# A 64-byte load on each DMA engine in front of the first tile's load of a gradient kernel

## Chip, cores, metric

One core of one Trainium2 chip. The metric is the device time of one execution in microseconds (us), median of several runs; lower is better. The profile's span is about 2 us shorter than that time and is used for everything inside the kernel.

## The reference

```python
def setup_inputs():
    return {"x": np.random.randn(8192, 8192).astype(np.float32)}

def reference(x):
    return np.gradient(x, axis=1)
```

Each output element is half the difference of its right and left neighbour in the row; the two end columns are plain differences. 268 MB are read and 268 MB written.

## The kernel before

The rows are cut into 32 tiles of 128 partitions x 2 rows (64 KiB per partition, 8 MiB in all), which pass through three slots. A slot starts with 64 spare elements, so that the result can be written 64 elements in front of the data it is made from.

```python
    R = 2; NB = 3; SH = 64; W = R * m; nsets = n // (P * R)          # 32 tiles
    slots = [pool.tile([P, SH + W], f32, ...) for k in range(NB)]
    ends = pool.tile([P, nsets, R, 2], f32, name="ends", tag="ends")

    def load(i):
        b = slots[i % NB]
        ins = nc.sync.dma_start(out=b[:, SH : SH + W], in_=x_sets[i])
        loads.append(chain(i, ins, *([stores[i - NB]] if i >= NB else [])))

    with tc.manual_schedule():
        for i in range(NB):
            load(i)                                   # loads 0, 1, 2
        for i in range(nsets):
            # GpSimd: the two end differences of each row into `ends`; waits for load i
            # VectorE: one custom instruction, half the neighbour difference, in place
            # VectorE or GpSimd: the ends into the result
            last = i == nsets - 1
            nr = 1 if last else R                     # the last tile goes in two halves
            for r in range(0, R, nr):
                ...
                ins = nc.sync.dma_start(out=out_sets[i, ...], in_=b[...])
                stores[i] = chain(i, ins, placed)
            if i % NB == NB - 1:                      # after every third tile
                for k in range(i + 1, min(i + 1 + NB, nsets)):
                    load(k)                           # each waits for the store of its slot
```

`chain` draws the dependences by hand.

Of the kernel before, what the change touches and what calls it, by code (L numbers as in the profile page):

```python
# [1 line left out]

# [4 lines left out]


@with_exitstack
def kernel(  # L10
    ctx: ExitStack,
    tc: tile.TileContext,
    x: bass.AP,
    out: bass.AP,
):










    nc = tc.nc
    P = nc.NUM_PARTITIONS
    n, m = x.shape
    R = 2
    NB = 3  # L30
    SH = 64
    W = R * m
    nsets = n // (P * R)
    f32 = x.dtype

    x_sets = x.rearrange("(s p t) m -> s p (t m)", p=P, t=R)
    out_sets = out.rearrange("(s p t) m -> s p (t m)", p=P, t=R)

    pool = ctx.enter_context(tc.tile_pool(name="pool", bufs=1))
    slots = [pool.tile([P, SH + W], f32, name=f"slot{k}", tag=f"slot{k}") for k in range(NB)]  # L40
    ends = pool.tile([P, nsets, R, 2], f32, name="ends", tag="ends")
    loads, stores = [], [None] * nsets
    in_front = {}

    def chain(i, ins, *needed):



        group, engine = f"slot{i % NB}", ins.ins.engine
        keep = [o.ins for o in needed]  # L50
        if in_front.get(engine, (None,))[0] == group:
            keep.append(in_front[engine][1])
        tc.declare_no_dep(ins.ins, group=group, keep=keep, reason="implied by the needed step")
        tc.add_to_no_dep_group(group, ins.ins)
        in_front[engine] = group, ins.ins
        return ins
# [4 lines that stand above are left out]
        loads.append(chain(i, ins, *([stores[i - NB]] if i >= NB else [])))  # L61

    with tc.manual_schedule():
        for i in range(NB):
            load(i)
        for i in range(nsets):
            b = slots[i % NB]
            xin = b[:, SH : SH + W].rearrange("p (t m) -> p t m", m=m)

            ins = nc.gpsimd.tensor_sub(  # L70
                out=ends[:, i, :, :],
                in0=xin[:, :, 1 : m : m - 2],
                in1=xin[:, :, 0 : m - 1 : m - 2],
            )
            at = [chain(i, ins, loads[i])]
            last = i == nsets - 1
            nr = 1 if last else R
            for r in range(0, R, nr):
                c0, c1 = r * m + 1, (r + nr) * m - 1

                ins = nc.vector._custom_dve(  # L81
                    dve_ops.TENSOR_TENSOR_REDUCE_SUB_MAX,
                    out=b[:, c0:c1],
                    in0=b[:, SH + c0 + 1 : SH + c1 + 1],
                    in1=b[:, SH + c0 - 1 : SH + c1 - 1],
                    s0=0.0,
                    s1=0.5,
                )
                halved = chain(i, ins, *at)
                res = b[:, r * m : (r + nr) * m].rearrange("p (t m) -> p t m", m=m)  # L90
                placer = nc.gpsimd if i % 5 in (1, 3) and not last else nc.vector
                ins = placer.tensor_copy(out=res[:, :, 0 : m : m - 1], in_=ends[:, i, r : r + nr, :])  # L92
                placed = chain(i, ins, halved)
                ins = nc.sync.dma_start(
                    out=out_sets[i, :, r * m : (r + nr) * m], in_=b[:, r * m : (r + nr) * m]
                )
                stores[i] = chain(i, ins, placed)
                at = [halved]
            if i % NB == NB - 1:
                for k in range(i + 1, min(i + 1 + NB, nsets)):  # L100
                    load(k)


# [1 line left out]
_INS = ['x']  # L105
_OUTS = [((8192, 8192), 'float32')]


# [23 lines left out]
```

## Time and profile before

| what | value | from |
|---|---|---|
| time | 1248.15 us median of 3 (1247.39 to 1248.5) | runs |
| span of the profiled run | 1245.0 us | page |
| VectorE busy | 45% | page |
| the DMA queue's packets | 99.8% of 16 engines' span | page |
| a 65,536-byte packet | 2.418 us, 512 per engine | packet records |
| first packets of load 0 | 3.10 us on the mean | packet records |

The kernel is one stream of packets on 16 engines. A packet is what one DMA engine moves in one go, in a load of a tile the 64 KiB of one partition. A 4-byte semaphore packet behind the last of them on each engine reports the end, and a transfer has *landed* when all 16 have done so. SPq is the queue of SyncE that issues transfers.

A line of stretches of time reads: start and end, length, VectorE busy (x instructions), GpSimd busy (x instructions), granted TensorE clock, DMA share, GB/s. A packet is counted with its whole length in the stretch in which it *starts*, so the DMA share can exceed 1, and the share times the length is how long the packets that start there last, per engine. The records do not name the engine of a packet; where the text tells engines apart, it goes by the order of the starts. The lines themselves stand in the prediction.

### The profile page before, as it was taken

The numbers are of one execution on the slowest core, as the hardware profiler recorded it, in microseconds if no ns is written. First come the engines' busy times: TensorE is split into PE (matmuls) and PEld (weight loads), VectorE is DVE, ScalarE is ACT, GpSimd is POOL, SyncE is SP. The second block draws the span as 40 slices with busy tenths as digits, with TensorE's granted clock in tenths as the row PEclk, the third lists the DMA queues.
The fourth block names the chain that finished last, engine by engine and source line by source line (L and its number), as shares of the span: only waits on it lengthen the run. The fifth ranks groups of instructions, "written<-read, shape, count | busy, mean of one in ns | idle before, by whom it ended". The sixth has DMA issues, their size and how long they took to land.

```text
span 1245.0 us, 241 instructions
## 1 busy us (share of the span) xinstructions
DVE 554.8 (45%) x54; POOL 8.8 (1%) x48
## 2 busy tenths in 40 slices
DVE  2850483079009603850582079009603840591083
POOL 0000000000000000000000000000000000000000
DMA  9999999999999999999999999999999999999999
GB/s 404 438 436 419 425 438 438 438 438 438 434 427 421 436 438 438 436 438 432 432 419 438 436 438 432 436 434 432 423 436 436 436 438 436 430 427 430 436 411 404
DMA packets 9361, 536.88 MB, mean 431 GB/s; under 512 B 1040, under 2 KB 1040, under 8 KB 1040
## 3 DMA queue, kind: packets, MB, share of 16 engines
q1 hardware_dynamic: 9360, 536.88, 99.8%
q14 instruction: 1, 0.01, 0.0%
HBM read 268.44 MB, written 268.44 MB: 431 GB/s over the span
## 4 chain that ended last, share of the span: by engine, by line
another core or an unknown queue 74%; DVE 18%; DMA 3%; issue 2%; POOL 1%; SPq 0%; POOLq 0%
DVE slot L81 18%; DMA slot<-in_x_dram 3%; POOL ends L70 0%; POOL slot L92 0%; SPq L60 0%; DVE slot L92 0%; POOLq L127 0%
## 5 line engine op out<-in xcount | busy, mean ns | idle before, releaser
L81 DVE CUSTOM_DVE_ANT_0 slot<-slot 128x16382 f32<-128x16382 f32 (+1 forms) x33 | 551.3, 16706 | 667.9 <-POOL ends L70 667.9
L70 POOL TENSOR_TENSOR ends<-slot 128x4 f32<-128x4 f32 x32 | 6.3, 198 | 988.8 <-DMA slot<-in_x_dram 988.8
L92 DVE COPY slot<-ends 128x4 f32<-128x4 f32 (+1 forms) x21 | 3.6, 172 | 0.7
L92 POOL COPY slot<-ends 128x4 f32<-128x4 f32 x12 | 2.3, 190 | 207.9 <-DVE slot L81 207.9
L116 POOL MEMSET const-bfloat16-1.0<- 128x1 bf16 x1 | 0.1, 102 | 0.0
L116 POOL MEMSET const-uint8-127<- 128x1 uint8 x1 | 0.1, 102 | 0.0
L116 POOL MEMSET const-float32-0.0<- 128x1 f32 x1 | 0.1, 99 | 0.2 <-issue 0.2
L116 POOL MEMSET const-float32-1.0<- 128x1 f32 x1 | 0.1, 99 | 0.0
## 6 DMA issues: line engine op xcount, KB each, us to landing
out_dram<-slot SPq DMA_DIRECT2D x2, 4096.0 KB, 20.2
slot<-in_x_dram SPq DMA_DIRECT2D x32, 58.0
out_dram<-slot SPq DMA_DIRECT2D x31, 40.3
```

The lines of the kernel that those rows point to most:

```text
L70: ins = nc.gpsimd.tensor_sub(out=ends[:, i, :, :], in0=xin[:, :, 1 : m : m - 2], in1=xin[:, :, 0 : m - 1 : m - 2],)
L81: ins = nc.vector._custom_dve(dve_ops.TENSOR_TENSOR_REDUCE_SUB_MAX, out=b[:, c0:c1], in0=b[:, SH + c0 + 1 : SH + c1 + 1], in1=b[:, SH + c0 ...
L92: ins = placer.tensor_copy(out=res[:, :, 0 : m : m - 1], in_=ends[:, i, r : r + nr, :])
L116: nc = _bacc.Bacc("TRN2", target_bir_lowering=False, num_devices=1)
```

## The change

The intent is to let a tiny transfer pay whatever the first transfer on each engine costs, so that the first big load starts at full speed. 16 rows of 64 bytes, one row for each engine; nobody reads them.

```diff
     ends = pool.tile([P, nsets, R, 2], f32, name="ends", tag="ends")
+    few = pool.tile([16, 16], f32, name="few", tag="few")
...
     with tc.manual_schedule():
+
+        nc.sync.dma_start(out=few[:], in_=x[0:16, 0:16])
         for i in range(NB):
             load(i)
```

## The prediction

> **What bounds the kernel now.** I read four views in this order: the page, the waits of the DMA-issuing engine, then stretches of time at the start, at the first store and near the end (with single packets of the trace where a mean was wanted). The page first:
>
> ```profile
> span 1245.0 us, 241 instructions
> ...
> DVE 554.8 (45%) x54; POOL 8.8 (1%) x48
> ...
> q1 hardware_dynamic: 9360, 536.88, 99.8%
> ...
> slot<-in_x_dram SPq DMA_DIRECT2D x32, 58.0
> out_dram<-slot SPq DMA_DIRECT2D x31, 40.3
> ```
>
> VectorE is busy 45% of the span, but one hardware queue holds packets on the 16 DMA engines 99.8% of it. The kernel is a stream of 32 loads and 32 stores (the last store in two halves). A load is 128 rows of 64 KiB, so each engine gets 8 packets of 65,536 bytes; all transfers together make 512 such packets per engine. In the packet records the usual packet takes 2.418 us (the median) and the next starts 2.416 us after it: 512 x 2.416 = 1237 us. Only some 8 us of the 1245 lie outside that, and the change can touch only a part of these.
>
> ```profile
> SPq L94 <- DVE slot L92: 525.7, 21, 55.9
> SPq L60 <- DMA out_dram<-slot: 373.2, 29, 19.2
> ```
>
> SyncE waits for long times, but not with the engines empty: when it waits for a store to free a slot, other transfers are queued (that is why a load takes a median of 58.0 us to land, three times its own 19.3 us). Inside the stream there is thus no idle time that could absorb a shift; a shift at the start goes through to the end. Now the start, in stretches. The last column times the length is the bytes of the packets that *start* in the stretch: 1165 x 0.9 us is 1.05 MB, 16 packets, one per engine.
>
> ```profile
> 0.74 1.33 SPq L60 DMA_DIRECT2D slot<-in_x_dram  x3
> 22.70 0.20 POOL L70 TENSOR_TENSOR ends<-slot 128x4 f32<-128x4 f32 x1 [22.26 <-DMA slot<-in_x_dram]
> ```
>
> ```profile
> 0.00:1.50 1.50, 0.00 (x0) 0.20 (x4) 1.00 0.00 0
> 1.50:2.40 0.90, 0.00 (x0) 0.00 (x0) 1.00 3.44 1165
> 2.40:4.50 2.10, 0.00 (x0) 0.00 (x0) 1.00 0.00 0
> 4.50:5.40 0.90, 0.00 (x0) 0.00 (x0) 1.00 2.69 1165
> 5.40:7.00 1.60, 0.00 (x0) 0.00 (x0) 1.00 0.00 0
> 7.00:7.80 0.80, 0.00 (x0) 0.00 (x0) 1.00 3.02 1311
> ```
>
> Load 0 is issued at 0.74 us; the engines' first packets start between 1.75 and 2.35 us (mean 1.92), the second between 4.62 and 5.37, the third between 7.04 and 7.79. So the first packets took 2.71 to 3.39 us, mean 3.10: **0.68 us more** than 2.42. That is also what the DMA share column shows: 3.44 x 0.9 = 3.10 us per engine against 2.69 x 0.9 = 2.42 for the second. This 0.68 us is the only thing that a load in front can save. (Loads 1 and 2 are issued 0.44 and 0.47 us after the one before.)
>
> A first store has such a cost too, and there the engines were not empty:
>
> ```profile
> 58.10:58.80 0.70, 0.70 (x1) 0.00 (x0) 1.00 4.82 1498
> 58.80:61.40 2.60, 0.69 (x1) 0.19 (x1) 1.00 0.00 0
> 61.40:62.20 0.80, 0.00 (x0) 0.00 (x0) 1.00 3.03 1311
> ```
>
> 4.82 x 0.7 = 3.37 us per engine (with the last load's 4-byte semaphore packets in it), about 0.95 more than 2.42; no later change from loads to stores shows it. A load does not touch this one.
>
> Near the end:
>
> ```profile
> 1186.42 17.23 DVE L81 CUSTOM_DVE_ANT_0 slot<-slot 128x16382 f32<-128x16382 f32 x1 [59.81 <-POOL ends L70]
> 1203.68 0.17 DVE L92 COPY slot<-ends 128x4 f32<-128x4 f32 x1
> 1203.88 19.93 SPq L94 DMA_DIRECT2D out_dram<-slot  x3
> ```
>
> Store 30 can be issued only when load 30 has landed (1186.2) and 17.2 us of VectorE have passed; most engines have then finished load 31 and stand idle, 1.49 us on average, until 1204.7. From there 16 packets per engine (38.7 us) run to 1243.7. This gap is set by when the *slowest* engine lands load 30, and it moves along with the loads, so it does not absorb a shift either.
>
> **What the Trainium skill says.** "DMA: Bandwidth & Descriptors", section "Why a DMA increments its semaphore by 16 and not by 1": the number of engines is the largest number up to 16 that divides the slowest dimension of both sides, so the 16-row load puts one 64-byte row on each of the 16 engines; the 128-row loads of before agree, with 16 first packets. The same page, section "Latency and other measured facts", gives about 600 ns to the first byte and about 800 ns as the least HBM round trip of a tiny transfer; the trace has 1.0 us from the issue to the first packet's start, and the extra 0.68 us of a first packet is of the size of such a trip. Section "Two DMAs through the same engine are not ordered" says that descriptors start in order but are pipelined; the trace agrees in that only the first packet of a long load shows the extra. Section "Where 436 GB/s comes from" puts the ceiling at 435.2 GB/s; 16 x 65,536 bytes per 2.416 us is 434, so the stream has nothing left to gain.
>
> **The change part by part.** It removes nothing. It adds:
> (a) One DMA issue on SyncE in front of load 0. At the measured spacing of first issues, 0.44 us, load 0's issue goes from 0.74 to about 1.18 us. Taking the same 1.0 us and the same spread, its first packets could start at 2.2 to 2.8 us instead of 1.75 to 2.35.
> (b) 16 data packets of 64 bytes and 16 semaphore packets of 4 bytes (9 ns each in the trace). The 64-byte ones start where load 0's first packets start now, 1.75 to 2.35 us. By its size one takes next to nothing; if it has the first packet's extra time, about 0.7 us (an estimate: the 0.68 us above), so they end at 2.45 to 3.05 us.
> (c) 64 bytes of SBUF on 16 partitions, which no instruction reads; no new wait. The DMA semaphores are used in turn, eight of them; every transfer still waits only for the one eight places before it, long done.
>
> If the small packet takes the extra time upon itself, load 0's first packet starts when both its descriptor and the engine are there, 2.45 to 3.05, and lasts 2.42: it ends at 4.87 to 5.47 us. Before, it ended at 4.75 to 5.32 or so. Sum: +0.44 (issue) + 0.26 (the small packet outlasts that by 0.70 - 0.44) - 0.68 (extra saved) = **+0.02 us** by the means, up to +0.14 by the ends of the ranges. So the small load pays the cost a little earlier and the issue slot eats the profit.
>
> **The rivals.**
> 1. *The extra is paid again*: it belongs to starting on an empty pipe, the small packet is gone before load 0's descriptor arrives, and load 0's first packet lasts 3.10 again. Then the whole 0.44 us of the issue is lost: +0.44 us, about 1248.6. For it: 64 bytes are quickly through. Against: the first store shows 0.95 with the pipe full, so the extra looks like a first use rather than an empty pipe.
> 2. *The small load is cheaper than I think*: few descriptors, so it starts at once everywhere, and its 0.68 lies wholly within the 0.44 and the descriptor latency. Then load 0's packets start at 2.2 to 2.8 and last 2.42: 0.44 - 0.68 = -0.24 us, about 1247.9.
> 3. *A small write stalls the engine*, or the semaphore packet behind it holds up the data: some 1 us more, 1249.2. Against: after load 0 the 4-byte packets take 9 ns and load 1 goes on without a gap.
> 4. *The stream falls otherwise into step*: the three runs of before differ by 1.1 us, and the engines' spread is about 2.6 us at load 31's end against 0.6 at the start. That is larger than the effect and can go either way.
>
> **Range and chances.** The cases lie between -0.24 and +1.0 us. I take mine and rival 1 as about equally likely and rival 2 as half as likely: (0.05 x 2 + 0.44 x 2 - 0.24) / 5 = +0.15, so 1248.15 + 0.15 = 1248.3 us. The scatter of the three runs (1247.39 to 1248.5) and of another session is more than this: I add about 1.3 us to each side, 1247.0 to 1249.6. Two per cent are 25 us; nothing in an opening of 5 us can make that. I leave half a per cent on either side.
>
> **What would show it right or wrong.** In the profile after: 32 packets more on the queue (9392); under 512 B 1072; the issue of the first big load about 0.44 us later; the 64-byte packets at about 1.75 to 2.35 us; 16 big packets starting between 2.2 and 3.1 us, and the next 16 at 4.7 to 5.6. If the two are 2.42 us apart, the small load took the extra on itself; if 3.1, rival 1 holds. Load 0's wait should end within 0.5 us of the 22.70 of before, and the first store should keep its 0.95. The prediction is wrong if the time moves by over 1.5 us, or if the shift at load 0 does not appear at the end in runs that are otherwise alike.

## The result

| | before | after |
|---|---|---|
| time, median (4 runs each) | 1248.33 us (1247.39 to 1248.68) | 1248.13 us (1247.87 to 1248.52) |
| span of the profiled run | 1245.0 us | 1246.0 us |

The ratio is 1.0 (95% interval 0.9983 to 1.0017). Ratios here are the mean time of one kernel's fast runs over that of the other's of the same rounds, so not quite the ratio of the medians. The times are the same; what the change did at the start has to be read from the profile. The page after, where it answers to the lines of before:

```profile
span 1246.0 us, 243 instructions
...
q1 hardware_dynamic: 9392, 536.88, 99.7%
...
few<-in_x_dram SPq DMA_DIRECT2D x1, 1.0 KB, 1.5
```

32 packets more, and the small load lands 1.5 us after its issue. The start in order of time, after:

```profile
0.74 0.39 SPq L66 DMA_DIRECT2D few<-in_x_dram  x1
1.18 1.36 SPq L61 DMA_DIRECT2D slot<-in_x_dram  x3
22.95 0.20 POOL L73 TENSOR_TENSOR ends<-slot 128x4 f32<-128x4 f32 x1 [22.51 <-DMA slot<-in_x_dram]
```

The small load takes load 0's place at 0.74 us; load 0 is issued 0.44 us later. The stretches of the start, after:

```profile
1.50:2.10 0.60, 0.00 (x0) 0.00 (x0) 1.00 0.03 2
2.10:3.20 1.10, 0.00 (x0) 0.00 (x0) 1.00 2.71 953
3.20:5.10 1.90, 0.00 (x0) 0.00 (x0) 1.00 0.00 0
5.10:5.70 0.60, 0.00 (x0) 0.00 (x0) 1.00 4.03 1748
```

In the first line are the small packets: 0.03 x 0.60 = 0.02 us per engine for a 64-byte packet and its semaphore packet (8 and 9 ns in the records; the 64-byte ones start at 1.75 to 1.91 us). In the second line are load 0's first packets, one per engine (953 x 1.1 us = 1.05 MB): 2.71 x 1.1 = **2.98 us** each, so still not 2.42. In the last line their successors start, at 5.49 us on the mean of the records against 5.01 before. The small load has saved nothing that can be seen of load 0's slow start, and load 0's data come **0.48 us later**. That is well beyond the scatter: in the seven profiles told of here in which load 0 is issued at 0.74 us, the second packets start at 4.98 to 5.07 us on the mean; in two profiles of the changed kernel at 5.49 and 5.50. The end of the first wait is a poorer measure, as it ends with the slowest engine: 22.95 against 22.70 us here, but 22.61 to 22.94 in those seven profiles.

### The profile page after: what moved, and what is told of

The parts are those of the page before. It is cut to its first block, busy times and chain, and to the rows that moved or that the text cites. A ratio compares the mean times of both kernels' runs of the same rounds, so it can differ in the third digit from the quotient of the medians.

```text
span 1246.0 us, 243 instructions
## 1 busy us (share of the span) xinstructions
DVE 554.8 (45%) x54; POOL 8.9 (1%) x48
## 4 chain that ended last, share of the span: by engine, by line
another core or an unknown queue 74%; DVE 18%; DMA 3%; issue 2%; POOL 1%; SPq 0%; POOLq 0%
DVE slot L84 18%; DMA slot<-in_x_dram 3%; POOL ends L73 0%; POOL slot L95 0%; SPq L61 0%; SPq L66 0%; DVE slot L95 0%; POOLq L130 0%
```

## The experiments

Two quantities are used throughout. The *lead* is the time from load 0's issue until its data flow at full rate: the mean start of the second packets, less one packet's 2.418 us, less the issue. The *rest* is the time from the mean start of the second packets to the end of the last packet of the kernel. In the kernel before the lead is 5.008 - 2.418 - 0.738 = 1.85 us and the rest 1238.7 us; after, 5.489 - 2.418 - 1.181 = 1.89 us and 1239.3 us. (In the seven profiles with load 0 at 0.74 us the lead is 1.83 to 1.91, so 0.04 us means nothing.) My theory after the first profile: the lead is a fixed cost of starting loads on idle engines, the small load only costs its issue slot, and the shift goes through to the end but is smaller than the scatter of the rest. The rivals: a first use that the small load might take on itself if placed or sized otherwise; a slowdown by the following loads' issues; a stream that absorbs the shift.

### Six small loads, and twelve

```diff
-        nc.sync.dma_start(out=few[:], in_=x[0:16, 0:16])
+        for j in range(6):          # or 12
+            nc.sync.dma_start(out=few[:, 16 * j : 16 * j + 16], in_=x[0:16, 16 * j : 16 * j + 16])
```

> Six small loads of 64 bytes per engine in front instead of one. Theory (the issue slot is all that the small load costs, the first packet's extra is not saved, and the shift goes through to the end): load 0 is issued 6 x 0.44 = 2.7 us later than in the kernel before, its landing ends the first wait at about 25.3 us (22.70 before, 22.95 with one), and the time rises by about 2.7 us, to about 1251. Rival (the stream absorbs shifts at the start, as the equal medians could also suggest): the landing moves by 2.7 us but the time by less than 1 us. Rival (small loads warm something up step by step): load 0's first packets last 2.42 us and the time rises by 2.0 us or less.

> Twelve small loads in front. Theory (0.44 to 0.46 us for each, nothing of it absorbed): load 0 is issued 5.4 us later than before, its second packets start at 10.4 to 10.5 us on the mean, and the time rises by 4.9 to 5.9 us. Rival (the stream absorbs part): the time rises by under 4 us. Rival (each small load costs more than its issue slot): over 6.5 us.

In order of time with twelve:

```profile
0.74 5.47 SPq L67 DMA_DIRECT2D few<-in_x_dram  x12
6.25 1.37 SPq L61 DMA_DIRECT2D slot<-in_x_dram  x3
28.29 0.20 POOL L74 TENSOR_TENSOR ends<-slot 128x4 f32<-128x4 f32 x1 [27.84 <-DMA slot<-in_x_dram]
```

| small loads | load 0 issued | second packets, mean | lead | ratio of time (95%) | in us |
|---|---|---|---|---|---|
| none | 0.74 us | 5.01 us | 1.85 us | 1 | 0 |
| 6 | 3.48 | 7.86 | 1.96 | 1.0026 (1.0014 to 1.0039) | +3.2 |
| 12 | 6.25 | 10.59 | 1.92 | 1.0042 (1.0030 to 1.0055) | +5.2 |

("In us" is the ratio less 1, times the median of before.) Twelve small loads shift load 0's data by 5.6 us and the time by 5.2 us; six by 2.9 and 3.2. Each small load costs 0.46 us of issue, and the stream passes the shift to the end. A stream that absorbs the shift is refuted by the six: it asked for under 1 us, and the interval is 1.7 to 4.9 us. With twelve the interval, 3.7 to 6.9 us, holds the shift of 5.6 but just reaches into both rivals (under 4 and over 6.5), so a partial absorption is made unlikely, not excluded; in the profiles the rest is 1238.7 us with none and with twelve. Small loads warm nothing up step by step either: after twelve the lead is still 1.92 us. The second packets were expected at 10.4 to 10.5 us; they came at 10.59, a small miss.

### The small load from another queue

```diff
-        nc.sync.dma_start(out=few[:], in_=x[0:16, 0:16])
+        nc.scalar.dma_start(out=few[:], in_=x[0:16, 0:16])
```

> The same small load issued by ScalarE's queue, so that SyncE's load 0 keeps its place at 0.74 us. Theory (only the issue slot costs): load 0's issue at 0.74 us, first packets of about 3.1 us, landing at 22.7 us as before, time as before within 0.1%. Rival (a first use that the small load takes on itself, eaten up by the issue slot): first packets of about 2.4 to 2.6 us, landing at about 22.0 us, time 0.6 us shorter.

Load 0 is back at 0.74 us, the small load is issued at the same moment by ScalarE, and load 0's second packets start at 4.99 us (5.01 before): lead 1.83 us. The first wait ends at 22.64 us; time 1248.11 us, ratio 0.9999 (0.9986 to 1.0011). Taken off the issue path the small load costs nothing and brings nothing. The records of load 0's first packets last 2.96 us here, a little less than I expected, only because some of them start later; the data do not come earlier. This is why the start of the second packet is the better measure. One thing this run does not test, though the expectation says so, is a first use: in the records the small packets start only at 4.62 to 5.35 us, behind load 0's first packets and not in front of them.

### The small load behind load 0

```diff
+        load(0)
         nc.sync.dma_start(out=few[:], in_=x[0:16, 0:16])
-        for i in range(NB):
+        for i in range(1, NB):
             load(i)
```

> The same small load between load 0 and load 1. Theory (only the issue slot in front of load 0 costs): landing of load 0 at 22.7 us as before, load 1 issued 0.44 us later but hidden behind load 0's 19 us, load 1 landing at 42.0 us as before, time as before within 0.1%. Rival (the extra packets themselves cost engine time): load 1 lands 0.2 us or more later than before.

The second packets start at 5.06 us, the waits for loads 0 and 1 end at 22.68 and 42.02 us (22.70 and 42.04 before); ratio 1.0003 (0.9990 to 1.0015). The 16 small packets pass between the two loads in 11 ns each. So the packets cost nothing; the place in front of load 0 does.

### Load 0 waits for the small load

```diff
-        nc.sync.dma_start(out=few[:], in_=x[0:16, 0:16])
+        small = nc.sync.dma_start(out=few[:], in_=x[0:16, 0:16])
         for i in range(NB):
             load(i)
+            if i == 0:
+                after(loads[0], small)        # load 0 waits until the small load has landed
```

(`after(a, b)` makes `a` wait for the landing of `b`. The later runs use it too.)

> Load 0 waits until the small load has landed (1.5 us from its issue in the profile after), so the engines have done a whole transfer and are idle again when load 0 comes. Theory (the extra belongs to every start of loads on idle engines, not to a first use): the small load's semaphore is full at about 2.25 us, load 0 is issued at about 2.3, its first packets last 3.0 to 3.1 us again, landing at 24.2 to 24.4 us, time about 1.6 us longer. Rival (a first use of engine, ring or memory that needs one finished transfer): first packets of 2.42 us, landing at about 23.6, time about 0.9 us longer.

The stretches of the start:

```profile
1.50:2.10 0.60, 0.00 (x0) 0.00 (x0) 1.00 0.03 2
2.10:3.20 1.10, 0.00 (x0) 0.00 (x0) 1.00 0.00 0
3.20:3.70 0.50, 0.00 (x0) 0.00 (x0) 1.00 6.21 2097
3.70:6.20 2.50, 0.00 (x0) 0.00 (x0) 1.00 0.00 0
6.20:6.80 0.60, 0.00 (x0) 0.00 (x0) 1.00 4.03 1748
```

Here every engine has finished a whole transfer, data and semaphore, before load 0 is issued at 2.24 us. Load 0's first packets last 6.21 x 0.50 = 3.10 us nevertheless, as with no small load at all, and the lead is 1.82 us. The idea of a first use that one finished transfer takes away is refuted. The wait ends at 24.08 us, a little before the 24.2 that I expected at the least, and the time is longer by a ratio of 1.0014 (1.0000 to 1.0028), about 1.7 us.

### A larger load in front

```diff
-    few = pool.tile([16, 16], f32, name="few", tag="few")
+    few = pool.tile([16, 2048], f32, name="few", tag="few")
...
-        nc.sync.dma_start(out=few[:], in_=x[0:16, 0:16])
+        nc.sync.dma_start(out=few[:], in_=x[0:16, 0:2048])
```

> One load in front as in the change, but of 8 KiB on each engine instead of 64 bytes: 0.3 us of transfer at the engines' full rate. Theory (fixed 1.85 us from issue to flow, for the load in front as for load 0): the load in front flows from about 2.6 to 2.9 us, load 0 from about 3.05; the second packets of load 0 start 0.45 to 0.6 us later than before; the 8 KiB packets carry an extra of about 0.7 us themselves (about 1.0 us each) and load 0's first packets carry less of it in their records, but nothing is gained; time as before within 0.1%. Rival (64 bytes are too little to warm an engine, 8 KiB are enough): load 0's second packets start at 5.0 us or sooner.

The 8 KiB packets last 0.32 to 0.59 us, not the 1.0 us that I expected, where full rate would take 0.30; so a small packet's record shows little of the slow start, and mine was the wrong idea of where it would appear. Load 0's second packets start at 5.50 us, as after the change; lead 1.90 us, ratio 1.0002 (0.9988 to 1.0016). More bytes in front do not help either.

### Loads on idle engines in the middle of the program

```diff
                     load(k)
+                    if k == NB:
+                        after(loads[k], stores[NB - 1])     # load 3 also waits for store 2
+                    elif k < 2 * NB:                        # second run only
+                        after(loads[k], loads[k - 1])       # loads 4 and 5 start singly
```

> The kernel before, with load 3 waiting also for store 2, so that loads 3, 4 and 5 are issued one behind the other on engines that have run dry in the middle of the program, 100 us after the first use of everything. Theory A (each start of loads on idle engines costs the extra): load 3's first packets last about 3.0 us, as at the start. Theory B (the extra comes from the next two loads being issued meanwhile): 3.0 us here too, but 2.42 us in the run with single issues. Theory C (something of the first microseconds of the program alone): 2.42 us. Time: engines idle for about 2 us once, plus the extra: 2.0 us longer under C, 2.6 to 2.7 under A and B.

> As the last, and loads 4 and 5 each wait for the landing of the load before, so that three loads start singly on idle engines in the middle. Theory A: the first packets of each last about 3.0 us; time three times 2.7 us, about 8 us longer. Theory B: 2.42 us each, time about 6 us longer. Theory C: 2.42 us each.

The stretches around the three single starts in the second run:

```profile
121.20:122.30 1.10, 0.00 (x0) 0.00 (x0) 1.00 2.83 953
122.30:124.30 2.00, 0.00 (x0) 0.00 (x0) 1.00 0.00 0
124.30:125.00 0.70, 0.00 (x0) 0.00 (x0) 1.00 3.46 1498
143.10:143.70 0.60, 0.60 (x1) 0.00 (x0) 1.00 5.31 1748
143.70:146.10 2.40, 2.40 (x1) 0.00 (x0) 1.00 0.00 0
146.10:147.00 0.90, 0.90 (x1) 0.00 (x0) 1.00 2.69 1165
```

2.83 x 1.10 = 3.11 us and 5.31 x 0.60 = 3.19 us for the first packets of loads 3 and 4, and 3.17 us for those of load 5 (records); the packets after them 2.42 us (2.69 x 0.90). With the three issued together it is 3.10 us. The three leads are 1.85, 1.86 and 1.88 us, the same as at the program's start. So the cost came back at **every** start of loads on idle engines that was tried, also 100 us after the first use of anything, and it does not come from the issues that follow. Theory A holds, B and C fall.

The ratios are 1.0032 (1.0018 to 1.0046) and 1.0071 (1.0057 to 1.0085), about 4.0 and 8.9 us. A said 2.7 and 8; both lie within the intervals (2.2 to 5.7 and 7.1 to 10.6 us), so the times do not show that anything is missing. The traces do have one more difference of about 1 us: the last packets of load 5, just before the stores behind it, last 3.53 and 3.44 us in the two runs, as those of load 2 do in the kernel before (3.37 us), while in the kernel before those of load 5 take 2.42 us and in the other profiles with no such idle start up to 2.78.

### The first loads issued singly

```diff
             load(i)
+            if i > 0:
+                after(loads[i], loads[i - 1])
```

> The kernel before, with load 1 waiting for load 0 and load 2 for load 1 at the start: load 0 is issued alone. Theory A: load 0's first packets last about 3.1 us as before, and those of loads 1 and 2 too; landing of load 0 at 22.7. Theory B: load 0's first packets last 2.42 us, landing at about 22.0. Theory C: load 0's 3.1 us, those of loads 1 and 2 2.42. Time two idle stretches of about 2 us longer, 4 to 5.5 us in all.

Load 0's first packets last 3.07 us though nothing else is issued until 22.68 us, those of loads 1 and 2 3.05 and 3.13; ratio 1.0043 (1.0029 to 1.0057), 5.4 us. Theory A again.

### The changed kernel once more

> The changed kernel itself once more, for a second profile and more times. Theory (a start of loads takes a fixed time of about 1.85 us from the issue until the data flow at full rate, and the small load only moves the issue by 0.44 us): second packets of load 0 start 0.45 to 0.55 us later than in the kernel before, on the mean of the engines; time within 0.1% of before, because the slowest engine's later delays scatter by more than that. Rival (a gain of the change that one profile hid): second packets at 5.01 us or sooner.

No edit. The second packets start at 5.50 us, as in the first profile of the change; lead 1.90 us; ratio 1.0003 (0.9990 to 1.0015), median 1248.46 us. The rest is 1240.7 us here against 1239.3 us in the first profile *of the same kernel*. That is the scatter in which 0.48 us are lost.

### The last tile but one in halves

```diff
-            last = i == nsets - 1
+            last = i >= nsets - 2
```

> The kernel before, with the last tile but one also worked and stored in halves, so that its first half is stored about 8.5 us sooner and the engines need not stand idle at about 1203 us. Theory (the slowest engine sets the end, and that one did not stand idle: it ended load 31 at 1205.05 us, after the others had started store 30 at 1204.73): the idle 1.5 us of the mean disappear, the engines end at different times, and the time falls by less than 0.5 us. Rival (that idle stretch lies on the path): the time falls by 1.5 us.

Near the end of the kernel before:

```profile
1238.00:1239.50 1.50, 0.00 (x0) 0.00 (x0) 1.00 0.81 350
1239.50:1241.00 1.50, 0.00 (x0) 0.00 (x0) 1.00 0.81 350
1241.00:1242.50 1.50, 0.00 (x0) 0.00 (x0) 1.00 1.57 677
1242.50:1244.00 1.50, 0.00 (x0) 0.00 (x0) 1.00 0.06 22
```

and with the halves:

```profile
1238.00:1239.50 1.50, 0.00 (x0) 0.00 (x0) 1.00 1.11 481
1239.50:1241.00 1.50, 0.00 (x0) 0.00 (x0) 1.00 0.61 262
1241.00:1242.50 1.50, 0.00 (x0) 0.00 (x0) 1.00 0.20 87
1242.50:1244.00 1.50, 0.00 (x0) 0.00 (x0) 1.00 0.20 87
1244.00:1245.50 1.50, 0.00 (x0) 0.00 (x0) 1.00 0.05 22
```

Before, 16 packets are in flight until 1243.5 us and all end within 0.2 us. With the halves only eight are in flight at 1241.0 us and four at 1241.5, and the last two packets end at 1245.0 and 1245.4 us. The idle time at 1203 us is gone (1.50 us per engine before, 0.00 here), yet the end is no earlier: the waiting of the other engines for the slowest has moved to the end. The ratio is 1.0001 (0.9987 to 1.0014), that is -1.6 to +1.7 us, which alone would not quite exclude the rival's gain of 1.5 us; what speaks against it is the trace.

No experiment points to a version that beats both kernels.

## Why the prediction was right, point by point

The time, 1248.3 us in a range of 1247.0 to 1249.6, was right: 1248.13 us, and 1248.46 us when measured again. The chance of a change of over 2% was rightly put near nothing. The mechanism that I had put first was not the right one, so that the number came out right is luck as far as that mechanism goes: the range of 2.6 us held my own case (1248.2), rival 1 (1248.6), rival 2 (1247.9) and rival 3 (1249.2) alike, and the time cannot tell them apart.

- **The stream has no idle time to absorb a shift.** Right. With six and twelve small loads the time rose by 3.2 and 5.2 us for shifts of 2.9 and 5.6 us.
- **(a) The issue slot, 0.44 us.** Right: load 0's issue went from 0.738 to 1.181 us.
- **(b) The 64-byte packets.** They start where I put them, from 1.75 us, but do not last 0.7 us: 8 ns. The step of the sum that failed is "- 0.68 (extra saved)". The extra is not a first use that one transfer takes from the next. It came back in full after a landed small load (3.10 us), and in the middle of the program (3.10 to 3.19 us). With nothing saved, and nothing lost to a small packet outlasting the issue, the sum is +0.44 instead of +0.02; measured at load 0: +0.48 and +0.49 us. Two slips in the sums changed little: load 0's first packets ended at 4.62 to 5.37 us before, not "4.75 to 5.32 or so", so the ends of the ranges would have given +0.25 and +0.10 and not "up to +0.14"; and the weighted mean takes 0.05 where the sum gave 0.02, and leaves rival 3 out.
- **Rival 1, "the extra is paid again",** is what happened. I had weighed it equally with my own case, so that the predicted figure, +0.15, lay between.
- **The argument against rival 1** was a misreading. I took the 3.37 us packets at 58.2 us for the first store. They are the 24th of each engine, and three loads make 24 packets of each: 1.92 + 3.10 + 22 x 2.416 = 58.2 us. So they are load 2's *last* packets. And "no later change from loads to stores shows it", from which I took the extra for a first use, is not so. The last packets before later changes are longer too in some places, only less so; at 639 us in the kernel before 1.89 x 1.5 = 2.84 us on the mean:

```profile
639.00:640.50 1.50, 1.50 (x1) 0.00 (x0) 1.00 1.89 699
```

In all thirteen profiles load 2's last packets take 3.33 to 3.80 us on the mean. So the 3.64 us after the change (I expected the extra of 0.95 us to stay, and it was 1.22) lie within the scatter; the run with the halves, whose start is that of the kernel before, has 3.59. That only the first packet of a long load shows an extra holds for load 0, then, and not for load 2.

- **Rival 2** (a gain) and **rival 3** (a stall by the small write): neither. Small packets pass in 8 to 11 ns with the semaphore packet behind.
- **Rival 4, scatter,** is why the times look equal. The rest of the stream took 1238.7 us before, 1239.3 and 1240.7 us in two profiles of the changed kernel, 1238.2 us with the small load on the other queue. I put these 2.5 us down to the differing delays of the slowest engine; the records do not name the engine, so this is not shown. That the change costs 0.44 us is shown at the start of the trace; in the time it is not resolved, and is inferred from the runs with six and twelve.

What stays open: what the extra 0.68 us of a start consists of, and why the last packets before a change from loads to stores take longer, by about 1 us after a start from idle and by 0.6 us or less at other changes. No run here tells what goes on inside an engine.

## What to carry to other kernels

A small load ahead of the first big one did not shorten the start of the big one, because the cost came back whenever loads started on idle engines; it took its issue slot of 0.44 us, and in a stream as full as this one such a shift reaches the end. Judge such a change by the moment at which data flow (here the start of each engine's second packet) and multiply it until its cost stands out of the scatter. And before filling a stretch of idle engines, look whether the slowest engine is idle in it: here it was not, and nothing was gained.

## What the Trainium skill lacked or had wrong

- "DMA: Bandwidth & Descriptors", section "Latency and other measured facts", gives about 600 ns to the first byte. The runs agree if one counts from the *end* of the issue instruction: 0.62 to 0.64 us to load 0's first packet in twelve of thirteen profiles, 0.73 us behind the 8 KiB load. (The prediction's 1.0 us counts from its start.) What the page lacks is the time to full rate: 1.82 to 1.96 us from the start of load 0's issue, in thirteen profiles.
- The same page does not say that the first packets of a load on idle engines last longer than the ones behind them, whatever went before: 64 KiB took 3.0 to 3.2 us on the mean against 2.42 us, at the program's start, after a finished small load, and in the middle of the program.
- No page has what SyncE pays for issuing one more small load ahead of a big one: 0.44 to 0.46 us.
- No page has the slow last packets of the loads before a change to stores: 3.33 to 3.80 us on the mean of 16 at the first change, 3.44 and 3.53 us on load 5 in the runs that start in the middle, up to 2.98 us at other changes, against 2.42 us.
